# Order of work, four projection tiles at once, and 128 bytes of padding in a two-layer hybrid encoder on one Trainium2 core

## The chip, the cores and the metric

The kernel runs on one core of one Trainium2 chip. Its engines work at the same time, each through its own queue in order: TensorE (PE, with PEld for the weight loads), VectorE (DVE), ScalarE (ACT), GpSimd (POOL) and SyncE (SP, which here only issues DMAs). PE writes to PSUM, which has eight banks of 128 x 512 float32; all else lives in SBUF, 128 partitions wide. The metric is the device time of one execution in microseconds, as a median over runs.

## The reference

A batch of one, 512 tokens, 1024 channels, two layers. Each layer does, in float32:

- `xn = RMSNorm(x)`, then one projection `z = xn @ w_in` whose columns are dealt out to three branches and three gates.
- Branch A: a gated linear recurrence with four heads of 128 x 128, forward and backward, then a per-head RMSNorm and a SiLU gate.
- Branch B: `gelu(u) * (W_s LayerNorm(gelu(v)) + b)`, with one 128 x 128 mixing matrix for each of four channel groups and each 128 tokens.
- Branch C: attention over a window of 128 to both sides, eight query heads on two key heads, rotary embedding of a quarter of each head, a learned sink logit in the softmax.
- Merge: each branch is projected to 1024 channels, multiplied by a sigmoid gate (columns of `z`), summed, projected by `w_out` and added to x.
- MLP: `x = x + relu(RMSNorm(x) @ w_up)**2 @ w_down`, with 4096 hidden channels.

After both layers comes a final RMSNorm with its weight.

## The kernel before

**Precision.** A product in float32 precision is made of three passes: each operand is split into a rounded part (hi, made on ACT) and the rest (lo, made on DVE), and PE adds hi*hi, lo*hi and hi*lo in PSUM. So 128 x 128 by 128 x 512 costs three matmuls, and each weight chunk of 128 x 1024 costs one ACT copy (L179) and one DVE subtraction (L181). The raw chunks come by DMA from one array `ws` in the order of use.

**Two ways to multiply.** `proj` (L189) makes one 128 x 512 output tile, channels by tokens, from the eight channel tiles of x: 24 matmuls that need all of x. `seven` (L378) makes a 512 x 1024 by 1024 x 1024 product, tokens by channels, from seven half-size products instead of eight (Strassen's scheme in Winograd's form): each of the seven has 24 matmuls; products 3, 5, 6 and 7 work on sums of quarters of x, which `left_sums` (L346) makes on DVE into the tiles `xs` (or `sh` in the MLP), and products 1, 2 and 4 on plain quarters. Product 1, 6, 5 and 3 accumulate in PSUM tag c, 2 in m, 7 and 4 in a; two banks each.

**Stages of a layer.** (1) bu, the u of branch B, four tiles by `project_bu` (L660): in layer 0 at the very start, in layer 1 after head 0. (2) Three runs of `seven` (L723): values of A and v of B, then the gates of C and A. (3) The branches: heads of A one behind another (`a_head` L505, about 60 us each, through one exponent tile `ex` with a single buffer); B (gelu, LayerNorm, mixing); C (`c_run` L916: for each of four head pairs and four token blocks, scores, softmax and output, chained through PE, DVE and ACT); and eight `merge_b` steps (L796), each a gate tile and a projected tile of B, 36 matmuls, multiplied and stored to DRAM. (4) The projections of A and C (y), the output projection (wo). (5) The MLP in four quarters: 8 `up` tiles, then one `seven` (`down`, L426). The last down run also adds the result to x, takes the row sums of squares for the next norm (`done`, L1021) and, in layer 0, turns x for layer 1.

**What sets the order.** A planner orders the instructions of each engine ahead of time from priorities, which follow the order of the program: `hp()` puts a block ahead, `later(n)` puts it n places back (C by 15000, merges and A's gates by 30000). Tiles of one tag share a fixed number of buffers and are handed out in turn, so a later tile of the tag waits for an earlier one. In the branch stage the program reads: head 0; gelu and B; head 1; C's keys, values and first two query tiles; merge 0; C run 0; head 2; merges 1, 2; C run 1; merge 3; head 3; merge 4; C run 2; merges 5 to 7; C run 3; the four gate projections of A.

**Start.** x arrives channels by tokens in eight tiles (L617), two bu weight chunks among them; POOL squares them, DVE adds the squares, PE sums over channels (`colsum`, L228) for the row scale, POOL raises to -1/2 (L242), PE and ACT spread it to `rb` (L316), by which every projected tile is multiplied as it is read.

**SBUF.** Pools are stacked: `cst` (constants), `sb` (tiles that live throughout: x and its parts, weights, small tiles), then pools opened and closed by stage (`wq`, `G`, `Y1`, `br`, `Y2`, `mlp`), which hold `xs`, `sh`, `yh`, `yl`, `mgh`, `mgl` and the branches' tiles. `sb` starts at byte 19968 of a partition and ends at 134528.

**End.** `n1.end()` makes the row scale of all four token tiles, eight DVE steps scale and weight them, and SP and ACT issue the eight outputs in turn (L1078).

Of the kernel before, what the change touches and what calls it, by code (L numbers as in the profile page):

```python
# [32 lines left out]
def _chunk_keys():  # L33

    res = []
    for l in range(DEPTH):
        res += [(l, "bu", i) for i in range(4)]
# [20 lines left out]
def trunk(tc, xT, xt, ws, vec, fnb, bsb, snk, wst, rope, cmask, amask, ident, out):  # L58
# [10 lines left out]
    sb = pool(name="sb", bufs=1)  # L69
    ps = pool(name="ps", bufs=4, space=bass.MemoryType.PSUM)  # L70
# [105 lines left out]

    def wsplit(raw):
        hi = sb.tile([P, CW], F32R, tag="wh", bufs=WB, name=nm("wh"))
        nc.scalar.copy(hi, raw)  # L179
        lo = sb.tile([P, CW], F32R, tag="wl", bufs=WB, name=nm("wl"))  # L180
# [12 lines left out]
    def proj_w(xs, name, w, koff=0):  # L193
# [5 lines left out]
        return pt  # L199

# [27 lines left out]
    def colsum(acc, last=None):  # L228

        pt = PT("s", "cs")  # L230
        for j in range(4):
            nc.tensor.matmul(pt[:, j:j + 1], acc[:, j * P:(j + 1) * P], ones_t, start=last is None or j == 0, stop=last is None)
        if last is not None:
            for j in range(4):
                nc.tensor.matmul(pt[:, j:j + 1], last[:, j * P:(j + 1) * P], ones_t, start=False, stop=j == 3)
        return pt

    def rstd_c(pt, n):
        t = SM("ms", 4)
        nc.vector.tensor_scalar(t, pt[:, 0:4], 1.0 / n, EPS, ALU.mult, ALU.add)  # L240
        r = SM("rs", 4)
        nc.gpsimd.tensor_tensor(r, t, mhalf_t, ALU.pow)  # L242
        return r
# [11 lines left out]
    def norm_feat(l, xf):  # L255

        n = Norm()
        n.xs, acc = [], None
        for k in range(KT):
# [3 lines left out]
            sq = T("z", "sq")  # L263
            nc.gpsimd.tensor_tensor(sq, xf[k], xf[k], ALU.mult)
            if acc is None:
                acc = sq
            else:
                a = T("z", "sqa")
                nc.vector.tensor_tensor(a, acc, sq, ALU.add)
# [3 lines left out]
        n.xf = xf  # L273
        n.rc = rstd_c(colsum(acc), D)
# [103 lines left out]
    def seven(raw, hs, name, on):  # L378
# [4 lines left out]
        def product(n, w, pts, start):  # L383
            for s_ in range(2):
                with hp():
                    hi, lo = wsplit(w[s_])
                for k2 in range(2):
                    k = 2 * s_ + k2
                    c = slice(k2 * S, (k2 + 1) * S)
# [812 lines left out]
```

## Time and profile before

| | us |
|---|---|
| median of three runs | 1835.13 (1834.61 to 1836.73) |
| the profiled execution | 1836.94 |
| its span, first to last instruction | 1835.2 |
| PE busy | 1743.1 |
| DVE busy | 1315.4 |
| ACT busy | 1009.2 |
| mean granted clock of PE | 0.978 of full |

The span is some 1.7 us shorter than the execution's own time. The share of busy time says which engine is the bound on average; what one stage loses is read from that stage. A matmul's row has its duration with the latency in it, about 0.39 us for 512 columns, while the next one starts 0.23 us later: in a full stream the distance of starts counts. The granted clock falls to half after pauses of PE, and the same matmuls then start 0.43 us apart.

### The profile page before, as it was taken

The page shows a single profiled execution, that of the slowest core. Times are in us where ns is not written, and L with a number is a line of the kernel's source. Part 1 is how long each engine was busy: PE and PEld are TensorE (multiplying, and loading weights), DVE is VectorE, ACT ScalarE, POOL GpSimd, SP SyncE. Part 2 cuts the span into 40 slices and gives each one's busy share as a digit, 9 for nine tenths or more (in the row PEclk, how much of TensorE's full clock was granted, in tenths as well). Part 3 has the DMA queues.
Part 4 walks back from the last instruction along what each step waited for, and adds up shares of the span by engine and source line. Part 5 has one row for each costly group of instructions (what it writes and reads, how often), then busy time and mean ns, then how long its engine had stood idle before and what let it go on. Part 6 is the DMA issues. An engine that isn't in the chain of part 4 may idle for free.

```text
span 1835.2 us, 21898 instructions
## 1 busy us (share of the span) xinstructions
PE 1743.1 (95%) x8032; PEld 1420.4 (77%) x8032; DVE 1315.4 (72%) x2006; ACT 1009.2 (55%) x1683; POOL 135.4 (7%) x183
## 2 busy tenths in 40 slices
PE   5999999998799999999989999999979999999997
PEld 3878888887587778888867888778867778878785
DVE  8687787678465767676897769878764666586867
ACT  5455656566523645454565567767663345545463
POOL 3011010110210000000010100100102000000000
PEclk7999999999899999999989999999999999999999
DMA  6231322221344242333324232121215352332321
GB/s 235 91 109 67 112 75 81 81 87 47 135 152 168 73 138 74 122 98 109 123 95 138 73 111 81 52 98 64 87 46 184 126 184 94 102 104 92 105 68 46
DMA packets 54698, 189.34 MB, mean 103 GB/s; under 512 B 7232, under 2 KB 7744, under 8 KB 54592
## 3 DMA queue, kind: packets, MB, share of 16 engines
q1 hardware_dynamic: 43776, 153.35, 24.7%
q0 software_dynamic: 10240, 33.56, 5.2%
q8 instruction: 63, 1.03, 0.2%
q10 hardware_dynamic: 576, 1.05, 0.1%
q14 instruction: 43, 0.35, 0.1%
HBM read 171.15 MB, written 16.78 MB: 102 GB/s over the span
## 4 chain that ended last, share of the span: by engine, by line
PE 59%; issue 21%; DVE 10%; ACT 7%; DMA 2%; POOL 0%; SPq 0%; POOLq 0%; DVEq 0%; ACTq 0%
PE up L185 3%; PE up L187 3%; PE up L186 3%; DVE wl L181 2%; PE dA L393 2%; PE y L213 2%; PE at L512 2%; PE y L215 2%; PE y L214 2%; PE dA L394 2%; PE dA L395 2%; PE gA L395 2%; PE gA L393 1%; PE gA L394 1%; PE wo L213 1%
## 5 line engine op out<-in xcount | busy, mean ns | idle before, releaser
L181 DVE TENSOR_TENSOR wl<-wr,wh 128x1024 fp32r<-128x1024 f32 x172 | 213.3, 1240 | 186.5 <-ACT wh L179 186.2
L179 ACT CAST wh<-wr 128x1024 fp32r<-128x1024 f32 x172 | 180.7, 1051 | 289.8 <-PE up L186 101.3
L179 ACT CAST wh<-wq 128x1024 fp32r<-128x1024 f32 x196 | 205.8, 1050 | 236.1 <-PE dA L394 54.1
L181 DVE TENSOR_TENSOR wl<-wq,wh 128x1024 fp32r<-128x1024 f32 x196 | 239.4, 1223 | 119.2 <-ACT wh L179 117.0
L185 PE MATMUL up<-xh,wh 128*128 128x512 f32 x512 | 199.5, 391 | 4.7 <-ACT wh L179 2.8
L186 PE MATMUL up<-xl,wh 128*128 128x512 f32 x512 | 199.8, 390 | 0.0
L187 PE MATMUL up<-xh,wl 128*128 128x512 f32 x512 | 198.6, 390 | 0.1
L185 PEld LDWEIGHTS up<-xh,wh 128*128 128x128 f32 x512 | 96.1, 188 | 27.7 <-ACT wh L179 5.3
L187 PEld LDWEIGHTS up<-xh,wl 128*128 128x128 f32 x512 | 96.1, 188 | 20.9 <-DVE wl L181 0.9
L186 PEld LDWEIGHTS up<-xl,wh 128*128 128x128 f32 x512 | 96.1, 188 | 19.9 <-DVE xl L225 0.3
L393 PE MATMUL dA<-wh,sh 128*128 128x512 f32 x256 | 102.0, 399 | 0.2
L394 PE MATMUL dA<-wh,sh 128*128 128x512 f32 x256 | 100.9, 394 | 0.0
L395 PE MATMUL dA<-wl,sh 128*128 128x512 f32 x256 | 90.5, 394 | 0.0
L554 DVE TENSOR_TENSOR ex<-ex 128x512 f32<-128x512 f32 x112 | 77.0, 706 | 7.1 <-ACT kt L529 6.6
L512 PEld LDWEIGHTS at<-qt,kt 128*128 128x128 f32 x448 | 58.3, 194 | 8.2 <-ACT kt L529 3.2
L512 PE MATMUL at<-qt,kt 128*128 128x128 f32 x448 | 60.6, 279 | 3.6 <-ACT kt L529 2.1
L393 PEld LDWEIGHTS dA<-wh,sh 128*128 128x128 f32 x256 | 48.1, 188 | 14.7 <-ACT wh L179 3.7
L242 POOL TENSOR_TENSOR rs<-ms,mhalf_t 128x4 f32<-128x4 f32 x13 | 15.7, 1210 | 587.5 <-DVE ms L240 578.0
L395 PEld LDWEIGHTS dA<-wl,sh 128*128 128x128 f32 x256 | 48.1, 188 | 11.3
L394 PEld LDWEIGHTS dA<-wh,sh 128*128 128x128 f32 x256 | 48.3, 189 | 10.8
L526 ACT ACTIVATE qt<-ex 128x512 f32<-128x512 f32 x56 | 37.9, 676 | 32.8 <-DVE ex L554 26.7
L185 PE MATMUL gz<-xh,wh 128*128 128x512 f32 x128 | 51.3, 400 | 3.0 <-ACT wh L179 3.0
(382 smaller groups left out, 4435.0 us busy)
## 6 DMA issues: line engine op xcount, KB each, us to landing
wr<-in_ws_dram SPq DMA_DIRECT2D x172, 512.0 KB, 3.3
wq<-in_ws_dram SPq DMA_DIRECT2D x112, 512.0 KB, 3.8
thd<-zt POOLq DMA_DIRECT2D x32, 256.0 KB, 2.7
th<-thd POOLq DMA_DIRECT2D x32, 256.0 KB, 4.4
mgd<-mg POOLq DMA_DIRECT2D x16, 256.0 KB, 2.4
mB<-mgd POOLq DMA_DIRECT2D x16, 256.0 KB, 3.9
x<-in_xT_dram SPq DMA_DIRECT2D x8, 256.0 KB, 7.2
xr<-in_xt_dram POOLq DMA_DIRECT2D x8, 256.0 KB, 4.8
```

Source lines behind the costliest of these rows:

```text
L179: nc.scalar.copy(hi, raw)
L181: nc.vector.tensor_tensor(lo, raw, hi.bitcast(F32), ALU.subtract)
L185: nc.tensor.matmul(pt, whi, xhi, start=first, stop=False)
L186: nc.tensor.matmul(pt, whi, xlo, start=False, stop=False)
L187: nc.tensor.matmul(pt, wlo, xhi, start=False, stop=last)
L213: nc.tensor.matmul(pts[t], xh, hi[:, c], start=k == 0, stop=False)
L393: nc.tensor.matmul(pts[p], xh[:, t], hi[:, c], start=start and k == 0, stop=False, skip_group_check=True)
L394: nc.tensor.matmul(pts[p], xl[:, t], hi[:, c], start=False, stop=False, skip_group_check=True)
L395: nc.tensor.matmul(pts[p], xh[:, t], lo[:, c], start=False, stop=k == 3, skip_group_check=True)
L512: nc.tensor.matmul(pt[:, c], kk(st), qq[:, c], start=True, stop=True)
L526: nc.scalar.activation(qt.rearrange(shp, b=nb, h=2), e_q, AF.Exp)
L554: nc.vector.tensor_tensor(o_ap, o_ap, ap_of(ex, i_, [[istep, 2]] + z), ALU.add)
```

## The change

- **Pools.** A tile of 128 x 32 floats in a pool of its own stands between `sb` and the pools of the stages.
- **Start of layer 0.** x tile 0 comes first, then the first bu chunk in two halves, then pairs of x tiles each followed by a bu chunk, then x again by rows (tokens by channels), all at high priority. The row scale comes from Squares with row sums on ACT over that copy; POOL's squares, DVE's additions and `colsum` are gone. `lower_bounds` takes its scratch tile from a tag of the branch pool.
- **bu.** `proj_four` makes the four tiles side by side in four PSUM banks (two of m, two of a): for each channel tile of x twelve matmuls. The chunks of `ws` for bu are laid out by channels of x. In layer 1 bu stands behind product 1 of the first `seven`, and the spreading of the row scale (`norm_rows`) ahead of that.
- **seven.** The order of products is an argument; the first run of a layer has 1, 7, 6, 2, 5, 4, 3. Both weight chunks of a product are split ahead of the first matmul that needs the second one's, reads follow per half, and with `apart` the last product is made one half after the other.
- **down.** In the last quarter the earlier quarters' sum is added to x first, and each product is then added to x straight from PSUM with its row scale (`nr2` holds the negative); `done` is told of every half tile.
- **End.** The final norm is made for token tiles 2 and 3, then for 0 and 1 (`finish`); the first halves of tiles 0 and 1 are multiplied by the weight ahead of that and scaled on ACT; SP issues all outputs.
- **Branches.** C's keys, values and all four query tiles come after B, then C run 0, head 1, C runs 1 to 3, merge 0, C's last output, head 2, merges 1 and 2, head 3, merges 3 to 7, A's gates.

```diff
+    pad = pool(name="pad", bufs=1)
     ps = pool(name="ps", bufs=4, space=bass.MemoryType.PSUM)
...
+    pad_t = pad.tile([P, 32], F32, name="pad_t")
+    nc.gpsimd.memset(pad_t, 0.0)
...
+    def proj_four(xs, name, *key):
+
+        pts = [PT(tag, name) for tag in ("m", "m", "a", "a")]
+        for i in range(4):
+            hi, lo = wload(*key, i)
+            for k2 in range(2):
+                k = 2 * i + k2
+                for f in range(4):
+                    c = slice(k2 * S + f * P, k2 * S + (f + 1) * P)
+                    mm3(pts[f], hi[:, c], lo[:, c], xs[k][0], xs[k][1], k == 0, k == KT - 1)
+        return pts
...
-            sq = T("z", "sq")
-            nc.gpsimd.tensor_tensor(sq, xf[k], xf[k], ALU.mult)
-            if acc is None:
-                acc = sq
-            else:
-                a = T("z", "sqa")
-                nc.vector.tensor_tensor(a, acc, sq, ALU.add)
-                acc = a
+        ss = SM("ss8", 8)
+        for j, x in enumerate(xrows):
+            nc.scalar.activation(T("jk", "jk"), x, AF.Square, accum_out=ss[:, j:j + 1])
...
-        n.rc = rstd_c(colsum(acc), D)
+        s = SM("s4", 4)
+        nc.vector.tensor_tensor(s, ap_of(ss, 0, [[2, 4]]), ap_of(ss, 1, [[2, 4]]), ALU.add)
+        n.rc = rstd_c(s, D)
...
-    def seven(raw, hs, name, on):
+    def seven(raw, hs, name, on, order=(1, 2, 6, 7, 5, 4, 3), between=None, apart=False):
...
+            if n == order[0] and between:
+                between()
...
-    def down(qd, raw, hs, acc, done):
+    def down(qd, raw, hs, acc, xr, r2, nr2, done, last):
...
+            if qd == 3:
+                r = r2 if sign > 0 else nr2
+                V.scalar_tensor_tensor(xr[t][fl], pt, r[:, t:t + 1], xr[t][fl], ALU.mult, ALU.add)
+                if which in ("P2", "P165", "P74", "P1653"):
+                    done(t, fl)
...
+        if qd == 3:
+            for fl in range(2):
+                for t in range(4):
+                    V.scalar_tensor_tensor(xr[t][fl], acc[t][fl], r2[:, t:t + 1], xr[t][fl], ALU.mult, ALU.add)
+        seven(raw, hs, "d", on, apart=last and qd == 3)
...
+    def x_load(k):
         t = T("l", "x")
-        with hp():
-            nc.sync.dma_start(t, xT[:, k])
+        nc.sync.dma_start(t, xT[:, k])
         x0.append(t)
...
+    with hp():
+        x_load(0)
+
+        raw, hi, lo = sb.tile([P, CW], F32, tag="wr", bufs=WR, name=nm("wr")), *whl()
+        for i in range(2):
+            c = slice(i * S, (i + 1) * S)
+            nc.sync.dma_start(raw[:, c], ws[CHUNK[(0, "bu", 0)], :, c])
+            split(raw[:, c], hi[:, c], lo[:, c])
+        ready[(0, "bu", 0)] = hi, lo
+        x_load(1)
+        for i in (1, 2, 3):
+            x_load(2 * i)
+            x_load(2 * i + 1)
+            ready[(0, "bu", i)] = wload(0, "bu", i)
+        for i in range(8):
+            t = T("tv", "xt")
+            nc.sync.dma_start(t, xt[:, i // 2, (i % 2) * S:(i % 2 + 1) * S])
+            x0r.append(t)
...
+            if u == 0:
+                seven(raw, hx, "t", on_tok, (1, 7, 6, 2, 5, 4, 3), (lambda: bu.extend(project_bu())) if l else None)
+            else:
+                seven(raw, hx, "g", on_gate(u - 1))
...
-        if l:
-            bu = project_bu()
         for i in range(4):
             gelu2(bu[i])
...
+        def head(h):
+            g = a_ffb(h)
+            q = evac(proj(xs, "q", l, "q", h), "q", "q")
+            oa.append(a_head(l, h, g, q, vt))
+
         prev = None
+        c_run(0)
+        head(1)
+        c_run(1)
+        c_run(2)
+        c_run(3)
         fill(0)
...
         with later(15000):
             c_out(*prev)
+        head(2)
+        fill(1, 2)
+        head(3)
+        fill(3, 4, 5, 6, 7)
...
+        def finish(ts):
+
+            ss = SM("s4", 4)[:, 0:2]
+            nc.vector.tensor_tensor(ss, ap_of(n1.ss, 2 * ts[0], [[2, 2]]), ap_of(n1.ss, 2 * ts[0] + 1, [[2, 2]]), ALU.add)
+            rc = rstd_c(ss, D)
+            for fl in range(2):
+                for i, t in enumerate(ts):
+                    if fl == 0 and ts[0] == 0:
+                        nc.scalar.activation(xr[t][fl], xr[t][fl], AF.Copy, scale=rc[:, i:i + 1])
+                    else:
+                        nc.vector.scalar_tensor_tensor(xr[t][fl], xr[t][fl], rc[:, i:i + 1], fn_t[fl], ALU.mult, ALU.mult)
+                    nc.sync.dma_start(out[:, t, fl * S:(fl + 1) * S], xr[t][fl])
...
-    for fl in (0, 1):
-        for t in (2, 3, 0, 1):
-            nc.vector.scalar_tensor_tensor(xr[t][fl], xr[t][fl], n1.rc[:, t:t + 1], fn_t[fl], ALU.mult, ALU.mult)
-            (nc.scalar if t % 2 else nc.sync).dma_start(out[:, t, fl * S:(fl + 1) * S], xr[t][fl])
...
         if kind == "bu":
-            return tproj(wi, col(B_U, a[0]))
+            return rows(wi, a[0] * 2 * P, np.arange(B_U, B_U + S))
```

More of the change, by code (lines that the diff above doesn't have):

```diff
@@ L225, in split @@
             nc.vector.scalar_tensor_tensor(lo, src, scale, hi.bitcast(F32), ALU.mult, ALU.subtract)
[L228 to L236, printed above, removed]
-    def rstd_c(pt, n):
[L239 to L242, printed above, removed]
+    def rstd_c(pt, n):
+        w = pt.shape[1]
+        t = SM("ms", 4)[:, 0:w]
+        nc.vector.tensor_scalar(t, pt, 1.0 / n, EPS, ALU.mult, ALU.add)
+        r = SM("rs", 4)[:, 0:w]
+        nc.gpsimd.tensor_tensor(r, t, mhalf_t[:, 0:w], ALU.pow)
         return r
@@ L412, in seven @@
[L412 to L426 removed]
+                    split_w.append(wsplit(w[s_]))
@@ L446, in lower_bounds @@
         V = nc.vector
[L447 removed]
+        m = T("a", "lbm")[:, 0:8]
         V.tensor_tensor(m, a, b, ALU.max)
```

157 lines of the change are left out of this document (63 added, 94 removed).

## The prediction

> **What bounds the kernel now.** I read the page first, then the busy times of stretches cut where the stages change, then the order of time inside the poor ones.
>
> The page's engine totals, and its 40 slices for TensorE and its granted clock:
>
> ```profile
> PE 1743.1 (95%) x8032; PEld 1420.4 (77%) x8032; DVE 1315.4 (72%) x2006; ACT 1009.2 (55%) x1683; POOL 135.4 (7%) x183
> ...
> PE   5999999998799999999989999999979999999997
> ...
> PEclk7999999999899999999989999999999999999999
> ```
>
> TensorE (PE) is the bound nearly everywhere; the holes are the first slice, the end of each layer's branches (slices 10, 11 and 30), the layer boundary (slice 21) and the end. The stretches (start:end, length, then busy time and count of PE, weight loads, DVE, ACT, POOL, then clock, DMA share, GB/s):
>
> ```profile
> 0.00:59.20 59.20, 37.65 (x112) 26.62 (x113) 47.74 (x82) 28.88 (x44) 14.83 (x17) 0.77 0.51 183
> ...
> 182.70:440.00 257.30, 252.69 (x1338) 215.82 (x1337) 199.29 (x363) 163.04 (x312) 24.99 (x24) 1.00 0.25 84
> 440.00:487.40 47.40, 32.93 (x149) 25.10 (x148) 20.81 (x70) 28.55 (x92) 2.73 (x4) 0.78 0.09 29
> ...
> 920.00:948.40 28.40, 22.79 (x95) 17.00 (x93) 27.41 (x47) 21.26 (x48) 7.10 (x9) 0.82 0.21 75
> ...
> 1057.40:1340.00 282.60, 276.08 (x1427) 233.67 (x1426) 226.90 (x407) 196.70 (x355) 27.83 (x28) 0.99 0.24 81
> 1340.00:1387.40 47.40, 33.92 (x172) 26.02 (x171) 24.43 (x77) 30.27 (x95) 2.90 (x5) 0.93 0.12 39
> ...
> 1821.90:1835.20 13.30, 0.01 (x1) 0.00 (x0) 7.77 (x14) 1.39 (x4) 1.01 (x1) 0.66 0.41 158
> ```
>
> Busy hides the rate. Full rate is read from the order of time on PE: each row is the first matmul of a product of 24; between the last two rows lie two products.
>
> ```profile
> 64.65 0.39 PE L393 MATMUL tB<-wh,xh 128*128 128x512 f32 x1
> ...
> 70.10 0.40 PE L393 MATMUL tA<-wh,xs 128*128 128x512 f32 x1
> ...
> 75.68 0.39 PE L393 MATMUL tC<-wh,xs 128*128 128x512 f32 x1
> ...
> 86.85 0.40 PE L393 MATMUL tC<-wh,xh 128*128 128x512 f32 x1
> ```
>
> With xh as the stationary operand 24 take 5.45 us, 227 ns each; with xs the next takes 5.58 and the two after it 11.17, 232 to 233 ns each. That difference is the first term.
>
> **Aligned pools.** From the tile sizes (each rounded up to 32 bytes): the sb pool starts on a multiple of 256 bytes and holds thirteen kinds of small tile of 4 x 32 bytes, one of 4 x 64, the rest multiples of 2048. Thirteen times 128 is six and a half times 256, so every pool opened after sb starts 128 bytes past a multiple of 256, and their tiles, multiples of 512, stay there. xh, xl and the cast weights lie in sb, ahead of that; xs, sh, yh, yl, mgh, mgl lie behind. The new tile of 32 floats, 128 bytes, moves them all onto a multiple. Matmuls with such an operand, counted from the code: the down products 7 x 24 x 8 = 1344, the products with sums of x 4 x 24 x 6 = 576, the A and C projections 384, the output projection 384, and B's 192. The last run in the branch stage, where the heads pace; the other 2688 at 5.2 ns are 14 us, on the path because PE is full there. Nothing in the trace says that the address is the cause and not the pool; below, nothing, above, 15 us; I take **-13**.
>
> The Trainium skill, "TensorE: Matmul & The Clock Gate", section "Back-to-back issue gap", speaks against this: it gives the spacing as a function of the moving columns and the clock, with no term for an address. By that rule the pad is worth nothing (rival 2 gives that time); two spacings at one width and one clock above do not fit it.
>
> **The start: x first, bu four at once, row squares from the token layout.** Order of time on PE, then the waits and groups of the first 60 us (of the tile view: shortest/median/longest ns):
>
> ```profile
> 6.91 0.80 PE L185 MATMUL bu<-xh,wh 128*128 128x512 f32 x1 [6.91 <-ACT xh L224]
> ...
> 16.09 0.63 PE L185 MATMUL bu<-xh,wh 128*128 128x512 f32 x1
> 16.52 0.63 PE L186 MATMUL bu<-xl,wh 128*128 128x512 f32 x1
> ...
> 59.21 0.39 PE L393 MATMUL tA<-wh,xh 128*128 128x512 f32 x1
> ```
> ```profile
> PE bu L185 <- ACT xh L224: 10.2, 3, 6.9
> PE bu L186 <- DVE xl L225: 7.2, 5, 3.6
> ```
> ```profile
> L225 DVE SCALAR_TENSOR_TENSOR xl<-x,vec_t,xh x8: 739/740/1530, 6.9 to 35.1; 128x512 fp32r<-128x512 f32 x8
> ```
> ```profile
> L222 DVE TENSOR_TENSOR xs<-sf,xs 128x512 fp32r<-128x512 f32 x8 | 7.8, 1006 | 0.5 <-ACT xs L221 0.5
> ...
> L269 DVE TENSOR_TENSOR sqa<-sqa,sq 128x512 f32<-128x512 f32 x6 | 5.8, 960 | 0.0
> ```
> ```profile
> L181 DVE TENSOR_TENSOR wl<-wr,wh 128x1024 fp32r<-128x1024 f32 x172 | 213.3, 1240 | 186.5 <-ACT wh L179 186.2
> ```
>
> Each bu tile waits for all of x, whose last split starts at 35.1. bu's 96 matmuls end at 59.2, bu and the first two products (144) at 70.1; at 227 ns they are 32.7 us. After: twelve matmuls can follow each x tile, and x is no longer queued behind weights of the next stage. PE's bound: start near 6.5, some 10 us at the cold spacing seen above (0.43 us, 23 matmuls), 121 more at 227 ns: 44. DVE's bound: of its 47.7 us in the stretch to 59.2 the seven sqa go (6.7), and with them POOL's squares, beside which xl took up to 1.53 for 0.74 (I count two of the eight so: 1.6) and xs 1.01, where the boundary's rows below show 0.64 (8 times: 2.9). That leaves 36.5, plus two weight splits of 1.24 (the row below); from 5 us on, it ends near 44 without a pause. Added and covered: eight loads of x by rows (2 MB, issued on SP ahead of the next weights; they are needed a product later, with DMA half idle), eight Squares on ACT, which was busy 28.9 of 59.2. If that cover is gone the row scale is late, bu's tiles hold banks m and a, and the product now second, in bank a, waits for them. Ends: 44 (both bounds), and 60 (DVE's order as poor as now). I take 51 for 70.1: **-19**.
>
> **The layer boundary: bu of layer 1 between the first product and the rest.** PE and DVE in order of time:
>
> ```profile
> 936.70 1.22 PE L393 MATMUL tB<-wh,xh 128*128 128x512 f32 x2
> ...
> 939.75 0.79 PE L394 MATMUL tB<-wh,xl 128*128 128x512 f32 x1 [1.41 <-DVE xl L222]
> ...
> 948.37 0.48 PE L393 MATMUL tA<-wh,xs 128*128 128x512 f32 x1
> ```
> ```profile
> 957.88 1.28 DVE L222 TENSOR_TENSOR xs<-sf,xs 128x512 fp32r<-128x512 f32 x2
> ```
>
> The second product stalls on the last transposed quarter of x (DVE 27.4 of 28.4 us busy), and runs 11.7 us for 5.45, cold. After, 96 matmuls (21.8 us) stand there, the first half of them on features already turned. They end near 954; but the next product is 7, which needs the second sums of all four pairs, ready at 959 before and later by bu's four splits and four reads (4 x 1.24 + 4 x 0.7, a plain pass in the tail's rows: 7.8) less what product 2 had asked for by then: 963. So some 5 us of stall return. Loss now about 12, gain **-7**, between 0 (all returns) and -12. The broadcast of the row scale moves ahead too: its matmuls wait for POOL's power in PE's queue, with all of bu's second half behind them; they were ready before 948 (product 2's end), which bu's order reaches only half way. The 21.8 us themselves move here from layer 1's branches.
>
> **Branches: C ahead, B's merge behind head 3.** The last read of head 3 (on), the PE groups between it and the branch projections, where those begin, and C's largest DVE group over the branch stage:
>
> ```profile
> 463.57 0.69 ACT L611 ACTIVATE on<-oT,vec_t 128x512 f32<-128x512 f32 x1 [3.24 <-PE oT L609]
> ```
> ```profile
> L907 PE MATMUL po<-pT,cvt 128*128 128x256 f32 x30 | 9.3, 447 | 2.3 <-ACT pT L903 2.2
> L902 PE MATMUL pT<-id_t,sc 128*128 128x128 f32 x30 | 6.4, 327 | 2.5 <-ACT yc L909 2.5
> L873 PE MATMUL sc<-k,q 128*128 128x384 f32 (+1 forms) x6 | 3.0, 503 | 1.1 <-DVE mx L876 1.1
> L874 PE MATMUL sc<-kl,q 128*128 128x384 f32 (+1 forms) x6 | 2.3, 380 | 0.0
> ```
> ```profile
> 487.69 1.19 PE L213 MATMUL y<-wh,yh 128*128 128x512 f32 x4 [0.75 <-ACT yh L221]
> ```
> ```profile
> 1364.30 0.69 ACT L611 ACTIVATE on<-oT,vec_t 128x512 f32<-128x512 f32 x1 [2.79 <-PE oT L609]
> ```
> ```profile
> L876 DVE CUSTOM_DVE_ANT_0 sc<-sc,cmask_t,snk_t 128x256 f32<-128x256 f32 (+1 forms) x32 | 17.3, 547 | 5.9 <-PE pT L902 4.9 <-PE sc L874 0.7
> ```
>
> After head 3 only C's serial chain is left: 24 us in layer 0, 23 in layer 1 (1387.4 less 1364.3), with no other matmul in the list, while the eight merges and four gate projections, pure filler, are spent by then. After, C runs under heads 1 and 2 and the filler under head 3. So the 24 us go, and the heads' own end sets the start of y. They run one behind another through their one exponent tile, from 182.7 to 464: 281 us against PE work of 257.3 + 47.4 less 19 idle and, as lone matmuls count their latency (po 447 ns), some 11 more = 275. So filler is no more than enough, and a few us return for A's last product and split, which then nothing covers. C's DVE work under the heads (17.3 us in the row, and its small steps) slows heads 1 and 2 about as much as the absent merges relieve head 3. The merges' stores move back on POOL's queue with them:
>
> ```profile
> mgd<-mg POOLq DMA_DIRECT2D x16, 256.0 KB, 2.4
> ```
>
> They land 2.4 us after issue and are read back two projections later, 40 us. Layer 0: **-18** (ends -26, where PE is the bound, and 0).
>
> In layer 1 bu's 21.8 us of PE leave the stage, but the heads took 307 us (1057.4 to 1364.3) with a DVE busy 227 of the first 283. If they keep that pace the stage goes from 330 to some 304, -26, of which 21.8 was only moved: **-4** (ends -22, where PE's own work bounds it: 330 less 21.8, 20 idle and some 14 of latency, and +8).
>
> **The last norm in halves.** DVE in order of time:
>
> ```profile
> 1821.25 1.39 DVE L436 TENSOR_TENSOR acc<-acc,dA 128x512 f32<-128x512 f32 x2 [1.73 <-PE dA L395]
> 1822.55 1.41 DVE L1025 SCALAR_TENSOR_TENSOR xr<-acc,r,xr 128x512 f32<-128x512 f32 x2
> ...
> 1826.30 5.39 DVE L1080 SCALAR_TENSOR_TENSOR xr<-xr,rs,fn 128x512 f32<-128x512 f32 x8 [1.12 <-POOL rs L242]
> ```
>
> From the last matmul to the end are 13.3 us. One read of 0.75 replaces four steps (-2), one Square fewer (-0.6), the eight scalings of 5.39 become two on DVE beside two on ACT (-3.5); four outputs on one queue give some 1.5 back. **-4.5** (ends -7 and -1). The eight additions of the earlier quarters move ahead of the last down stage, where DVE has room; uncovered they cost 8 x 0.7. The new product orders and the smaller steps I put at nothing for the same reason, between -2 and +3.
>
> **Sum.** -13 -19 -7 -18 -4 -4.5 = -65.5. The profiled execution took 1836.9 (span 1835.2 and 1.7 around it), 1.8 above the median; 1836.9 - 65.5 = 1771.4, and as a median **1769.6**. The distances to the terms' ends, squared, added and rooted, are 22 below and 28 above: 1748 to 1798; for the likeliest alone I take the inner two thirds, 1755 to 1788.
>
> **Rivals.** (1) *PE stays the bound in both branch stages*: the heads gain from the quieter PE and end before the filler. For it: no hole from 182.7 to 440; against: the heads' 281 and 307 us. Layer 0 -26, layer 1 -22: 1744. Chance 0.17. (2) *The pad does nothing*, the spacing being the pool's and not the address's: 1783; 0.10. (3) *C's work on DVE and ACT slows the heads*: DVE is already at 77% and 80% in these stretches; 12 us more a layer: 1794; 0.16. (4) *Slower: filler left to the end is exposed.* Projections go out in program order through two weight buffers, and five merges (180 matmuls) and four gates (96) stand behind head 3's. If head 3's projections hold them until its z tile is free and C starves PE meanwhile, 276 x 0.227 = 63 us follow the heads. Then y of layer 0 starts at 464 + 63, +39, and layer 1's stage is 304 + 63 + 21.8 against 330, +59; less the 43.5 gained elsewhere: 1890. It decides from 36 us exposed a layer. Against: merges already stand in that order behind the heads' projections, and PE idles only 4.6 us from 182.7 to 440. Chance 0.05. (5) The gains cancel: 0.02. The forecast has 0.50.
>
> **Numbers.** Range 1738 to 1798: it is the terms' ends, stretched below to hold rival 1; it leaves out rival 4 and the tails of 1 and 3. Under 0.2% (3.7 us) I call no change. Faster 0.93, same 0.02, slower 0.05.
>
> **What would show it.** Products with xs, sh, yh at 227 ns; y of layer 0 within 6 us of head 3's last read, with no po or pT between; product 7 of the first merge ending near 51; a stall of about 5 us at product 7 after bu in layer 1; 9 us from last matmul to end. It is wrong if the heads take over 290 us in layer 0, if merges run after head 3's last read, or if the products with xs keep 232.

## The result, and the profile after

The changed kernel takes **1804.4 us** (median of four, 1802.91 to 1804.86) where the kernel before, timed beside it, takes 1834.87: 30.5 us less, ratio 0.9836 with a 95% interval of 0.9817 to 0.9855. The forecast was 65.5 us less, 1769.6, with a range of 1738 to 1798. It is faster, by 0.47 of what was forecast, and 6.4 us above the range's upper end. The profiled execution's span is 1802.2, 33.0 below that of before.

The page of the changed kernel, engine totals and the two lines of 40 slices:

```profile
PE 1713.4 (95%) x8024; PEld 1411.0 (78%) x8024; DVE 1300.1 (72%) x2005; ACT 1014.7 (56%) x1704; POOL 128.6 (7%) x177
...
PE   5999998999899999999999999899988999999997
...
PEclk9999999999899999999999999999999999999999
```

The deep holes at the end of the branches are gone; what is left there is a 9 or an 8. So the time did not stay as idle PE in one place. The busy times of the stretches that answer those of the prediction:

```profile
0.00:48.00 48.00, 27.15 (x105) 21.87 (x106) 30.22 (x53) 26.49 (x49) 4.75 (x10) 0.96 0.74 269
171.70:440.00 268.30, 257.95 (x1374) 218.90 (x1373) 206.71 (x424) 182.15 (x377) 26.72 (x24) 1.00 0.24 79
440.00:471.20 31.20, 22.54 (x114) 19.01 (x112) 15.62 (x28) 14.68 (x40) 1.89 (x3) 0.81 0.11 35
...
1340.00:1359.70 19.70, 10.88 (x55) 8.93 (x55) 8.41 (x17) 9.18 (x28) 1.78 (x3) 0.75 0.08 27
```

At the start PE is busy 27 of 48 us, and the DMAs 74% of it. In layer 0's branches PE now idles 10.4 us from 171.7 to 440 (4.6 before) and 8.7 after that.

The stages, from the first matmul of each in the order of time on PE. "Without pad" is the changed kernel less the added tile (an experiment below); its difference to before is what the rest of the change did, and stands against the forecast's terms without the pad's 13.

| stage | before | after | without pad | difference without pad | forecast |
|---|---|---|---|---|---|
| start to head 0's first projection, layer 0 | 182.7 | 171.7 | 173.4 | -9.3 | -19 |
| branches, layer 0 | 305.0 | 299.5 | 299.5 | -5.5 | -18 |
| y and output projection, layer 0 | 96.1 | 96.4 | 97.8 | +1.7 | 0 |
| MLP, layer 0 | 342.2 | 341.4 | 343.7 | +1.5 | 0 |
| layer 1's start, to head 0's projection | 131.4 | 147.7 | 149.8 | -3.4 beside bu's 21.8 | -7 |
| branches, layer 1 | 330.0 | 303.0 | 303.2 | -5.0 beside bu's -21.8 | -4 |
| y, output projection, layer 1 | 96.0 | 95.9 | 97.8 | +1.8 | 0 |
| MLP, layer 1 | 338.5 | 336.9 | 338.7 | +0.2 | 0 |
| last matmul to the end | 13.3 | 9.7 | 9.6 | -3.7 | -4.5 |

The last column but one sums to -21.7, the forecast to -52.5. The pad adds 11.3 by these traces. Two rows hold most of the gap: the start, 9.7, and layer 0's branches, 12.5.

**The start.** Order of time on SP (its DMA issues) in the changed kernel:

```profile
1.18 0.42 SPq L178 DMA_DIRECT2D wq<-in_ws_dram  x1
1.65 0.42 SPq L633 DMA_DIRECT2D x<-in_xT_dram  x1
2.11 3.86 SPq L178 DMA_DIRECT2D wq<-in_ws_dram  x7
6.02 0.61 SPq L642 DMA_DIRECT2D wr<-in_ws_dram  x1
...
10.73 7.21 SPq L633 DMA_DIRECT2D x<-in_xT_dram  x7
```

and on PE, the first matmul of a product in each row (the last three products have 24 matmuls and no wait in them):

```profile
17.02 0.80 PE L193 MATMUL bu<-xh,wh 128*128 128x512 f32 x1 [17.02 <-ACT wh L241]
...
47.96 0.39 PE L396 MATMUL tA<-wh,xh 128*128 128x512 f32 x1
...
53.40 0.39 PE L396 MATMUL tC<-wh,xs 128*128 128x512 f32 x1
...
59.50 0.39 PE L396 MATMUL tA<-wh,xs 128*128 128x512 f32 x1
...
64.94 0.39 PE L396 MATMUL tB<-wh,xh 128*128 128x512 f32 x1
...
70.38 0.39 PE L396 MATMUL tA<-wh,xs 128*128 128x512 f32 x1
```

The eight `wq` tiles of the first merge, 4 MB that PE does not use before 48, went out ahead of seven of the eight x tiles and of bu's first chunk. bu begins at 17.0 instead of near 6.5, and bu with two products is done at 59.5, where the forecast had 51 and the kernel before 70.1. The products with xs now take 5.44 us, 227 ns a matmul.

**The end of layer 0's heads.** On ACT and PE in order of time:

```profile
469.83 0.69 ACT L623 ACTIVATE on<-oT,vec_t 128x512 f32<-128x512 f32 x1 [2.99 <-PE oT L621]
```
```profile
471.15 2.07 PE L233 MATMUL y<-wh,yh 128*128 128x512 f32 x4 [1.36 <-ACT yh L241]
473.02 0.63 PE L234 MATMUL y<-wh,yl 128*128 128x512 f32 x1
473.45 0.63 PE L235 MATMUL y<-wl,yh 128*128 128x512 f32 x1
```

y begins 1.3 us after head 3's last read, with no work of C between: the order does what it was said to do. But that read stands 298 us after head 0's first projection, 281 before. The heads themselves got 17 us longer.

The first four matmuls of y take 2.07 us here; the same row of the kernel before, in the prediction, has 1.19. From 471.15 to 476.0 the granted clock is 0.50, and the matmuls start 0.43 us apart, as the last two rows do; in the first 4.3 us of y before it was 1.00. Before, the stretch at half the clock fell on the end of head 3 and on C's tail, and was over when y began.

### The profile page after: what moved, and what is told of

Read it like the earlier page. It is cut to its first block, busy times and chain, and to the rows that moved or that the text cites. A ratio compares the mean times of both kernels' runs of the same rounds, so it can differ in the third digit from the quotient of the medians.

```text
span 1802.2 us, 21912 instructions
## 1 busy us (share of the span) xinstructions
PE 1713.4 (95%) x8024; PEld 1411.0 (78%) x8024; DVE 1300.1 (72%) x2005; ACT 1014.7 (56%) x1704; POOL 128.6 (7%) x177
## 4 chain that ended last, share of the span: by engine, by line
PE 51%; DVE 6%; ACT 5%; issue 5%; DMA 1%; SPq 0%; POOL 0%; DVEq 0%; POOLq 0%; ACTq 0%
PE up L195 6%; PE up L193 6%; PE up L194 6%; PE dA L396 3%; PE dA L397 3%; PE dA L398 3%; PE dC L396 2%; PE dC L397 2%; PE dC L398 2%; DVE wl L189 2%; ACT wh L188 1%; PE y L233 1%; PE at L524 1%; PE y L234 1%; PE y L235 1%
## 5 line engine op out<-in xcount | busy, mean ns | idle before, releaser
L189 DVE TENSOR_TENSOR wl<-wr,wh 128x1024 fp32r<-128x1024 f32 x171 | 209.6, 1225 | 182.5 <-ACT wh L188 181.8
L193 PEld LDWEIGHTS up<-xh,wh 128*128 128x128 f32 x512 | 96.1, 188 | 26.7 <-ACT wh L188 4.5
L195 PEld LDWEIGHTS up<-xh,wl 128*128 128x128 f32 x512 | 96.1, 188 | 22.1 <-DVE wl L189 2.5
L194 PEld LDWEIGHTS up<-xl,wh 128*128 128x128 f32 x512 | 96.1, 188 | 21.2 <-DVE xl L245 1.8
L524 PEld LDWEIGHTS at<-qt,kt 128*128 128x128 f32 x448 | 57.7, 192 | 12.5 <-ACT kt L541 6.6
L253 POOL TENSOR_TENSOR rs<-ms,mhalf_t 128x4 f32<-128x4 f32 (+1 forms) x14 | 18.0, 1287 | 606.1 <-DVE ms L251 585.2
L398 PEld LDWEIGHTS dA<-wl,sh 128*128 128x128 f32 x256 | 47.9, 188 | 10.3 <-DVE wl L189 0.2
```

What stands on the lines that cost most here:

```text
L189: nc.vector.tensor_tensor(lo, raw, hi.bitcast(F32), ALU.subtract)
L193: nc.tensor.matmul(pt, whi, xhi, start=first, stop=False)
L194: nc.tensor.matmul(pt, whi, xlo, start=False, stop=False)
L195: nc.tensor.matmul(pt, wlo, xhi, start=False, stop=last)
L398: nc.tensor.matmul(pt, xh[:, t], lo[:, c], start=False, stop=k == 3, skip_group_check=True)
L524: nc.tensor.matmul(pt[:, c], kk(st), qq[:, c], start=True, stop=True)
```

## The experiments

Differences are those of medians against the changed kernel, each first taken against the kernel before that was timed beside it. The 95% interval of one such step is some 3 us to either side, so a difference of two is uncertain by 4 to 5 us. Stage lengths come from the traces, one profiled execution each.

**1. The pad alone, on the kernel before.**

```
+    pad = pool(name="pad", bufs=1)
...
+    pad_t = pad.tile([P, 32], F32, name="pad_t")
+    nc.gpsimd.memset(pad_t, 0.0)
```

> The kernel before with nothing but the added tile of 32 floats. Theory (the forecast's term): the stationary operand's start address sets the spacing, every product with xs, sh, yh goes from 232 to 227 ns, and since PE is full, 2688 such matmuls give -13 us. Second theory (from the two traces: a down quarter went from 83.9 to 83.2 us only, y and the output projection not at all): the spacing goes to 227 ns, but about half of the gain is taken back by waits for weight splits, -4 to -7 us. Rival: the spacing belongs to something else that the change did, 232 ns stays, 0 us.

1820.58 against 1836.37 us: -15.8, ratio 0.9923 (0.9906 to 0.994). The same products as in the prediction's order of time on PE:

```profile
64.66 0.39 PE L397 MATMUL tB<-wh,xh 128*128 128x512 f32 x1
...
70.10 0.39 PE L397 MATMUL tA<-wh,xs 128*128 128x512 f32 x1
...
75.54 0.39 PE L397 MATMUL tC<-wh,xs 128*128 128x512 f32 x1
...
86.42 0.39 PE L397 MATMUL tC<-wh,xh 128*128 128x512 f32 x1
```

5.44 us a product with xs in place of 5.58. The first theory holds, nearly all of the gain reaches the end (14.8 us by the traces); the rival that the pad does nothing falls.

**2. The pad taken out of the changed kernel** (the same lines removed).

> The changed kernel with the added tile of 32 floats taken out again, all else as it is. Theory of the forecast: +13 us against the changed kernel, 232 ns. Second theory: 232 ns and +4 to +7 us. Rival: 227 ns and 0 us.

1814.05 us, +8.2, +11.3 by the traces. Between the two theories' numbers: in the changed kernel the pad is worth some 8 to 11 us, alone some 15 to 16. The medians alone do not tell these apart; by the stages, the pad gives 0.2 us in the two branch stages of the changed kernel and gave 3.7 in those of the kernel before. That a faster matmul gives less where the heads pace PE is a reading of these stages, not a test.

**3. What the address does.** A kernel of nothing but 16 blocks of 96 matmuls, one after another, behind one block to warm up; it was timed once.

```
for b in (0, 32):                              # moving operand, floats past a multiple of 64
    for a in (0, 8, 16, 32, 48, 64, 96, 128):  # stationary operand
        block(a, b, 96, ...)
```

> Not the model: 96 matmuls of 128x512 in a row for each of eight start addresses of the stationary operand (0, 32, 64, 128, 192, 256, 384 and 512 bytes past a multiple of 256) and two of the moving one (0 and 128 past it); nothing else is computed. Theory (the stationary operand's address modulo 256): 227 ns at 0, 256 and 512, 232 ns at 128 and 384, whatever the moving one's; between them unknown. Rival (the moving operand's address, or the pool and what else runs): the eight agree within 1 ns, or the two columns differ.

Stretches of 18 us inside the blocks, with the count of PE's matmuls (cut ones at both edges included): stationary at 0, at 128 and at 256 bytes with the moving one at 0, then stationary at 0 and at 128 with the moving one at 128:

```profile
33.00:51.00 18.00, 18.00 (x81) 14.90 (x80) 0.00 (x0) 0.00 (x0) 0.00 (x0) 1.00 0.00 0
...
99.00:117.00 18.00, 18.00 (x79) 14.62 (x78) 0.00 (x0) 0.00 (x0) 0.00 (x0) 1.00 0.00 1
...
143.00:161.00 18.00, 18.00 (x81) 14.92 (x80) 0.00 (x0) 0.00 (x0) 0.00 (x0) 1.00 0.00 1
209.00:227.00 18.00, 18.00 (x79) 14.49 (x78) 0.00 (x0) 0.00 (x0) 0.00 (x0) 1.00 0.00 0
...
276.00:294.00 18.00, 18.00 (x81) 14.90 (x80) 0.00 (x0) 0.00 (x0) 0.00 (x0) 1.00 0.00 1
```

Mean distance of starts in ns, by the stationary operand's bytes past a multiple of 256. With the moving operand at 0, 256 and 512 agree with 0, and 384 with 128, within 0.3 ns. With it at 128, 384 agrees with 128 (226.8 and 226.9), but 256 and 512 gave 232.4 where 0 gave 233.3; this 0.9 ns is not explained:

| moving at | 0 | 32 | 64 | 128 | 192 |
|---|---|---|---|---|---|
| 0 | 227 | 233.3 | 233.4 | 232.4 | 228.9 |
| 128 | 233.3 | 233.4 | 229.0 | 226.9 | 233.4 |

Both accounts miss in part. It is neither operand's own address but the difference of the two (stationary less moving), modulo 256 to within that 0.9 ns: 0 gives 227, 128 gives 232 to 233, 192 gives 229, 32, 64 and 160 give 233. Two operands both at 128 run at full rate.

**4. x and bu first on SP.**

```
-                with hp():
+                if key == (0, "un", 0):
                     nc.sync.dma_start(t, ws[CHUNK[key + (i // 2, i % 2)]])
+                else:
+                    with hp():
...
```

> The changed kernel, but the eight weight loads of layer 0's first merge lose their high priority, so that SP issues x and bu's weights first. Theory (SP's queue order is what cost the start): the first bu matmul at 7 to 8 us instead of 17.0, the two first products done near 51 instead of 59.4, -7 to -9 us against the changed kernel, the rest as it is. Rival (DVE's splits pace bu anyway): bu starts early but waits between the x tiles, the two products still end at 58 to 60, 0 us.

1794.53 us, -11.4 against the changed kernel, -9.4 by the traces, where 7 to 9 were expected. SP and PE in order of time:

```profile
1.18 0.42 SPq L636 DMA_DIRECT2D x<-in_xT_dram  x1
1.65 0.42 SPq L645 DMA_DIRECT2D wr<-in_ws_dram  x1
...
3.06 4.49 SPq L636 DMA_DIRECT2D x<-in_xT_dram  x7
...
16.15 5.31 SPq L178 DMA_DIRECT2D wq<-in_ws_dram  x8
```
```profile
6.65 2.07 PE L196 MATMUL bu<-xh,wh 128*128 128x512 f32 x4 [6.65 <-ACT wh L244]
```

bu begins at 6.6 and ends at 31.1, so DVE's splits do not pace it; the gate runs begin 9.5 us earlier (77.5 for 87.0) and layer 0's branches 11.1. The seven products of the first run now take 46.4 us for 39.0, so part of what bu wins is waited for there, which the forecast's bound from DVE's list covers. From before, head 0's first projection moves by 22.1, of which the pad has 1.7: the forecast's -19 was about right for the order that the change's text asks for, and the planner made another.

**5. Head 1's projections ahead of C's.**

```
+        head(1)
         def rot(z):
...
         c_run(0)
-        head(1)
```

> The changed kernel with head 1's projections and gates placed ahead of C's six projections (as they were before), C's four runs and the fillers as they are. Theory (the order of the projections cost the heads in layer 0): head 0's period goes from 64 back to 52 us, y of layer 0 begins some 10 to 12 us earlier, layer 1 within 3 us, -8 to -12 us in all. Rival (the recorded rival 3: C's work on DVE and ACT slows whatever head it lies under): head 0 and 1 gain, heads 2 and 3 lose as much, y begins within 3 us of where it does now, 0 us.

1809.29 us, +3.4; layer 0's branches 304.8 us for 299.5. The theory falls: what slows the heads is not the order of projections on PE. The rival's mechanism is left, though the stage is 5.3 us longer where it said 0.

**6. The same, and C's preparation with late priority.**

```
+        with later(15000):
             ck = evac(proj(xs, "ck", l, "ck"), "ch", "ck")
...
             cv = T("ch", "cvt")
             nc.scalar.copy(cv, pt)
```

> The changed kernel with head 1's projections first, as in the run with head 1 ahead, and C's projections, rotation and key splits given the late priority that its runs already have, so that the engines' queues hold the heads' steps ahead of them. Theory (C's steps on DVE and ACT stand ahead of the heads' in the queues): heads back to about 281 us in layer 0, -8 to -15 us against the run with head 1 ahead, and below the changed kernel. Rival (the queues' order does not matter, the engines' sums do): within 3 us of the run with head 1 ahead, +5 us against the changed kernel.

1806.15 us, -0.3 against the changed kernel and 3.7 below the run before this one, where 8 to 15 were expected; layer 0's branches take 304.9 us, as without it. The theory's gain is not there: a lower priority does not take the steps out of the way.

**7. The old order of the branches back in the changed kernel.**

```
+        g1 = a_ffb(1)
+        q1 = evac(proj(xs, "q", l, "q", 1), "q", "q")
+        oa.append(a_head(l, 1, g1, q1, vt))
...
+        fill(0)
         c_run(0)
-        head(1)
+        head(2)
+        fill(1, 2)
         c_run(1)
...
```

> The changed kernel with the branch stage put back: head 1 ahead of C, two of C's query projections up front, C's runs and B's merges spread over heads 1 to 3 as before (bu of layer 1 stays at the boundary). Theory of the forecast: the new order is worth 18 + 4 us, so this is 22 us slower than the changed kernel. Second theory (from the two traces): the heads took back in layer 0 17 of the 24 us that C's chain had cost after them, so the order is worth some 11 us in all, +8 to +13. Rival: bu's move to the boundary made layer 1's gain and the order made none there, +5 us or less.

1818.13 us, +11.7: the second theory's number. But the stages say more: layer 0's branches take 311.9 us, 12.4 more than with the new order and 6.9 more than in the kernel before, whose order this is. So the new order gives 12.4 us in layer 0, and some other edit takes about 7 there. From head 0's first projection to head 3's last read, and from there to y, in us:

| | layer 0: heads | to y | layer 1: heads | to y |
|---|---|---|---|---|
| kernel before | 280.9 | 24.1 | 306.9 | 23.1 |
| before, with the pad | 280.8 | 23.3 | 304.2 | 23.0 |
| changed, old order | 288.5 | 23.4 | 282.1 | 23.3 |
| changed | 298.2 | 1.3 | 301.7 | 1.3 |

The order takes 22 us of C's tail away in both layers, and its work under the heads costs them 9.7 us in layer 0 and 19.6 in layer 1. Once bu has left layer 1's branches, its heads drop by the whole 22 us of bu; the new order takes most of that back. By the traces the run is 14.6 us longer than the changed kernel; 5.4 of this lie ahead of layer 1's heads, where the matmuls are the same and 2.6 us are a wait for POOL's row scale, so that the median falls on the second theory's number is partly chance.

**8. C's rotation left out** (five tiles a layer; nothing replaces it).

```
         def rot(z):
-            sh = T("g", "sh")
...
             return z
```

> The changed kernel with C's rotation left out (five tiles a layer, each one shuffle, two passes on DVE and one on POOL; it changes what is computed, and nothing else is taken out). Theory (recorded rival 3: C's small work on DVE and ACT stands in the queue ahead of the heads' own chain): ten DVE passes of 0.7 us less in layer 0's stage of 299.5 us, most of it in the 36.7 us between head 0's last level and head 1's first, so that gap falls by 3 us or more and y of layer 0 begins 3 to 8 us earlier. Rival (the heads are paced by TensorE, which is full there): the gap and y's begin stay within 1.5 us.

1785.98 us, -20.5 (-16.5 by the traces); the branches take 292.9 and 295.1 us for 299.5 and 303.0. The size is the theory's, the place is not: the gap after head 0 falls only from 36.7 to 34.7 us, the rest lies in the heads' levels. Fifteen DVE passes of 0.7 us (the five shuffles are DVE's too) and five POOL passes cost 7 to 8 us of the heads' pace a layer. That this work of C slows the heads, as the recorded rival 3 has it, is shown for the changed kernel; how much of it the kernel before had paid as well was not run.

**9 and 10. The rotation's POOL pass to DVE, and its DVE passes to POOL.**

```
-            nc.gpsimd.tensor_tensor(z, z, cos_t, ALU.mult)
+            nc.vector.tensor_tensor(z, z, cos_t, ALU.mult)
```

> The changed kernel with one of the rotation's passes (the product with the cosines, POOL, 1.3 to 2.2 us, five a layer) moved from POOL to DVE. Theory (a POOL pass stretches the DVE pass beside it, 677 ns to 1464 to 1785, so it costs DVE more than it saves): five DVE passes of 0.7 us more, five stretches of 0.8 to 1.1 us fewer a layer, and C's prep shorter by a us a tile: 1 to 6 us faster. Rival (only DVE's own list counts): 5 x 0.7 us a layer more at the 0.8 us per us that leaving the rotation out gave, 4 to 6 us slower.

> The changed kernel with the rotation's product with the sines and its sum moved from DVE to POOL, so that three POOL passes follow one another and DVE keeps the shuffle alone. Theory (as above): ten DVE passes of 0.7 us fewer a layer, but ten more POOL passes of 1.5 to 2 us, each of which stretches what runs beside it on DVE by about its half: no gain, within 3 us, or slower. Rival (only DVE's own list counts): most of what leaving the rotation out gave, 8 to 14 us faster.

With the cosine product on DVE 1795.43 us, -10.3 (-7.3 by the traces): more than the theory's 1 to 6. With all but the shuffle on POOL 1811.33, +5.6 (+8.3 by the traces). The rival, DVE's own list alone, is wrong in sign both times. Duration of the product with the sines (shortest, median, longest ns), first in the kernel before, then changed, then with the cosine product on DVE:

```profile
L825 DVE TENSOR_TENSOR sh<-sh,sin x10: 676/682/1792, 231.4 to 1315.9; 128x512 f32<-128x512 f32 x10
```
```profile
L852 DVE TENSOR_TENSOR sh<-sh,sin x10: 677/1464/1785, 201.1 to 1124.5; 128x512 f32<-128x512 f32 x10
```
```profile
L852 DVE TENSOR_TENSOR sh<-sh,sin x10: 685/691/700, 201.1 to 1119.6; 128x512 f32<-128x512 f32 x10
```

The median went from 682 ns to 1464, because three of the ten were stretched in the kernel before and seven in the changed one, where C's tiles are rotated in one go; none is over 700 once POOL has no pass of the rotation. Every stretched one began while POOL's product with the cosines was running, and ended 0.54 to 0.55 us after that product's end, as if it had waited for it. The three that began up to 0.24 us ahead of POOL's product took 686 to 691 ns. The Trainium skill, "GPSIMD Engine Reference", section "Specifications", says that GpSimd shares its SBUF interfaces with VectorE and contends with DVE instructions that have two SBUF inputs; the rows agree. One thing stays open: by the traces the gain is all in layer 0's branches (292.9 us for 299.5); layer 1's take 303.6 for 303.0.

**11. The lower bounds back at the start.** After the old order still took 7 us too long, the trace of the changed kernel showed this on ACT, inside head 1's levels of layer 0:

```profile
277.68 1.28 ACT L481 ACT_TABLE_LOAD   x1
278.97 0.21 ACT L481 ACTIVATE lb<-lb 128x8 f32<-128x8 f32 x1
279.20 1.28 ACT L905 ACT_TABLE_LOAD   x1
...
281.70 1.28 ACT L481 ACT_TABLE_LOAD   x1
282.99 0.21 ACT L481 ACTIVATE lb<-lb 128x8 f32<-128x8 f32 x1
...
283.62 1.28 ACT L538 ACT_TABLE_LOAD   x1
```

and in the kernel before the same logarithm stood in the first 11 us:

```profile
L469 ACT ACTIVATE lb<-lb x2: 194/202/210, 8.2 to 10.5; 128x8 f32<-128x8 f32 x2
```

The change gives one scratch tile of 128 x 8 to ring a of the branch pool. That ring belongs to the heads, so the tile waits for head 0, and the whole calculation with it.

```
-        m = T("a", "lbm")[:, 0:8]
+        m = SM("lb", 8)
```

> The changed kernel with the lower bounds' first small tile taken from the ring of small tiles of sb, which is free at the start, instead of from ring a of the branch pool. Theory (that tile's new ring moved the whole calculation, with four table loads of 1.28 us on ACT, from the first 13 us into head 1's levels, 269.6 to 283.2): head 1's levels fall by 5 us or more, y of layer 0 begins 5 to 8 us earlier, nothing changes in layer 1, -5 to -8 us. Rival (the heads of layer 0 are held by C's preparation alone, and the table loads lie in ACT's idle time): y begins within 2 us, 0 us.

1797.7 us, -6.2; layer 0's branches 293.7 us for 299.5. Head 1's levels, first to last, with the bounds at the start and then in the changed kernel (busy PE, weight loads, DVE, ACT, POOL):

```profile
269.80:301.90 32.10, 31.83 (x180) 27.45 (x179) 25.83 (x54) 24.31 (x47) 3.82 (x3) 1.00 0.16 58
```
```profile
268.10:306.40 38.30, 32.57 (x181) 27.46 (x180) 28.06 (x71) 29.82 (x55) 2.94 (x3) 1.00 0.14 49
```

Six us, with 5.5 us more of ACT in the second. The theory holds; that ring a, and no other wait, held the tile is read from the code, and this run and the next agree with it.

**12. That one edit alone, on the kernel before.**

```
-        m = T("jk", "lbm")[:, 0:8]
+        m = T("a", "lbm")[:, 0:8]
```

> The kernel before with that one edit of the change alone: the lower bounds' first small tile from ring a of the branch pool instead of ring jk. Theory: the calculation moves from the first 13 us into head 1's levels, which take 43 instead of 36 us, +5 to +8 us, some of it given back at the start. Rival: 0 us.

1843.02 against 1834.33 us: +8.7, ratio 1.0047 (1.0031 to 1.0063); layer 0's branches 309.9 us for 305.0. Its shortest execution, 1840.76, is longer than the longest of the kernel before, 1838.04.

**13. bu of layer 1 behind head 0 again**, still four tiles at once.

```
-                ... (lambda: bu.extend(project_bu())) if l else None)
+                ... None)
...
+        if l:
+            bu = project_bu()
```

> The changed kernel with layer 1's four bu tiles back behind head 0's projections instead of between the first merge's first two products. Theory of the forecast: the boundary term of 7 us is lost and the branches gain nothing from it, +7 us. Second theory (from the two traces: net of bu's 21.8 us the stage from the boundary to the branches is 5.5 us shorter and the branch stage 5.2): +3 to +7 us, since part of the branch stage's gain stays. Rival (bu's 21.8 us fill the holes at the end of layer 1's heads, 15 us idle there): 5 us faster or more.

1843.75 us, +38.0: no account had that. The four tiles hold both banks of tag a, which every step of a head needs. In order of time on PE, head 0's last transposes and then bu:

```profile
1102.43 1.12 PE L621 MATMUL oT<-id_t,ao 128*128 128x128 f32 x4 [3.33 <-DVE ao L617]
1103.20 0.78 PE L193 MATMUL bu<-xh,wh 128*128 128x512 f32 x1
```

As the trace reads, bu waits for head 0's last bank, head 0 runs alone, and head 1's first level begins at 1202.9, 120 us after head 0's last (31 to 37 us between layer 0's heads of the changed kernel). So bu four at once and its move belong together; the run does not price the place by itself.

**14 and 15. The fixes together**: x first with the cosine product on DVE, then these two with the lower bounds at the start.

> The changed kernel with x and bu's weights first on SP and the cosine product on DVE: both edits together. Theory: they lie in different stages and add, -9.9 us from the start and what the cosine run gives beside it, 1788 to 1794 us. Rival (what the start gains is lost again in the heads): 1800 or more.

> The changed kernel with three edits: x and bu's weights first on SP, the cosine product on DVE, and the lower bounds at the start. Theory (they add): 1787.3 of the run with the first two, less 5 to 8, 1779 to 1783 us. Rival (the start then holds the lower bounds' small steps on DVE, which paces it, or the heads' gain overlaps with the cosine's): 1785 to 1790 us.

1787.34 us (ratio 0.9736, 0.9721 to 0.975, to the kernel before) and 1788.17 us (0.9744, 0.9726 to 0.9763). The first is 18.4 below the changed kernel, where its two edits alone gave 11.4 and 10.3: they add, nearly. The third does not show on top: layer 0's branches fall from 294.2 to 292.1 us, not by 5.8, and the times agree within their spread. The lower bounds and POOL's pass may in part have been the same wait; no run shows it. Both beat the kernel before and the changed one.

## Why the prediction was wrong

**Right:** *aligned pools*. The spacing fell as said, and -13 was between what the pad does alone (-14.8 to -15.8) and in the changed kernel (-8 to -11). The stated cause, the operand's place modulo 256, was nearly right: it is the place relative to the moving operand.

**Failed: the start's step "x is no longer queued behind weights of the next stage".** It was taken from the order of the program; the planner put the first merge's loads ahead, and bu waited until 17.0. The term -19 came out at -9.3; with SP's order mended it is -20.4 without the pad: bu and two products' worth of matmuls, 144, are then out by 48, four us past the two bounds of 44, and a part of what that wins is lost again to the weight splits of the products behind.

**Failed: the branches of layer 0, and there the sentence that put "the smaller steps" at nothing.** One of them, the lower bounds' scratch tile, moved a calculation by some 270 us into the heads: 5 to 6 us. The order itself was mis-sized: -12.4 in place of -18. The step "C's DVE work slows heads 1 and 2 about as much as the absent merges relieve head 3" does not hold: head 3 was not relieved, from its first level to its last read it took 63 us for 57, and the heads paid 9.7 us for the order (the table of experiment 7), 6.7 of them between head 0's last level and head 1's first, where C's preparation stands in one go beside POOL. Rival 3 had the mechanism and nearly the price, 12 us; I gave it 0.16. By the forecast's own test, over 290 us for the heads, it is wrong. Of the 17 us that the heads lost, 9.7 are thus the order's and 5.6 to 5.8 the lower bounds'; the other 2 are not settled, nor is what slows head 3. The cosine product on DVE alone gives the heads 6.6 us back, and with all fixes together they still take 290.8.

**Mis-sized: the layer boundary,** -3.4 in place of -7 without the pad. The stall of 5 us at product 7 did not come; one of 3.7 came later. Busy times of layer 1's first run in three stretches and of the first gate products:

```profile
909.00:931.00 22.00, 22.00 (x99) 18.14 (x99) 20.01 (x39) 12.93 (x25) 6.35 (x5) 0.92 0.40 137
931.00:955.00 24.00, 23.80 (x106) 19.42 (x104) 19.91 (x26) 15.01 (x21) 0.00 (x0) 1.00 0.26 88
955.00:972.90 17.90, 17.84 (x79) 14.46 (x77) 14.69 (x16) 7.04 (x8) 0.00 (x0) 1.00 0.47 147
972.90:1000.00 27.10, 23.37 (x102) 18.24 (x103) 26.59 (x40) 16.69 (x23) 4.32 (x6) 1.00 0.30 97
```

PE is full through product 7; in the gates it loses 3.7 us beside a DVE busy 26.6 of 27.1 (0.1 us in the same place before, with DVE busy 18.5 of 26.2), because with bu there early the work on B's tiles starts there too. That cause is read from the trace, not tested.

**Right in size by luck: the branches of layer 1,** -5.0 for -4. The forecast let the heads keep their 307 us without bu and gave C's 23 us away. They kept 302, but by two moves that cancel: bu's leaving took 22 us off them, and C's work under them put 19.6 back. **Right in size:** the last norm, -3.7 for -4.5.

**Left out: the clock at y's begin.** y and the output projection lost 1.7 and 1.8 us without the pad, because y's first matmuls now run at half the clock, and that stretch fell on the end of head 3 and on C's tail before. In the run with head 1 ahead the clock is 1.00 when y begins, and the stage takes 94.1 us for 96.4, as with the pad alone. Layer 0's MLP lost 1.5, for which no run gives the cause. Together these are +5, where the small steps were put between -2 and +3.

## What to carry to other kernels

Where a planner or a ring of buffers decides the order, the program's text does not say when an instruction runs: for each load and each renamed scratch tile ask which queue and which ring hands it out, and what stands ahead there. An edit that is "nothing" by its own length can carry a chain of waits and table loads into the one stretch that paces the kernel. And where one serial chain paces a stage, work moved under it from other engines' idle time is not free: price it by what it does to that chain's neighbours on DVE and ACT.

## What the runs showed of the hardware

The distance between matmuls of 128x512 depends on where the stationary operand lies relative to the moving one, modulo 256 bytes: 227 ns at 0, 229 at 192, 232 to 233 at 32, 64, 128 and 160, all at a granted clock of 1.00; 96 and 224 were not run. The Trainium skill, "TensorE: Matmul & The Clock Gate", section "Back-to-back issue gap", gives the spacing by columns and clock alone; the measurement differs, and decides. For this kernel 128 bytes are worth 8 to 16 us. And a DVE pass of two SBUF inputs (the product with the sines) that began while a POOL pass of two (that with the cosines) was running ended 0.54 to 0.55 us after it, at 1150 to 1792 ns for 682, so that moving that pass from POOL to a busy DVE made the kernel 7 to 10 us faster.
